# Two units of modulation columns later in attention, and one matmul for an input's hi and lo halves

## The chip, the cores and the metric

The kernel runs on one core of a Trainium2 chip, in one launch. The metric is device time in microseconds of that launch; the number for the kernel before is the median of three runs. One further execution was profiled, and all rows below come from it.

## What is computed

A sequence of 256 tokens of width 1024, in float32, goes through two blocks. The first has two layers; each is a mixer and an MLP with a squared ReLU, both modulated by a conditioning vector `c`. Layer 0 mixes by pooling, layer 1 by attention of 16 heads of 64 (with one key block of 256 it is causal attention with a relative-position bias):

```
mod = silu(c) @ w_mod[i] + b_mod[i];  sh1, sc1, g1, sh2, sc2, g2 = split(mod, 6)
h = rmsnorm(x) * (1 + sc1) + sh1
x = x + g1 * mixer(h)                       # layer 1: softmax(q k^T / 8 + bias) v, then @ w_o
h = rmsnorm(x) * (1 + sc2) + sh2
x = x + g2 * (relu(h @ w_up[i]) ** 2) @ w_down[i]          # d_ff = 4096
```

The second block has a gated delta rule and a forgetting attention side by side over 16 + 256 tokens, and then

```
h = h + (silu(f @ w_gate) * (f @ w_up)) @ w_down,   f = rmsnorm(h)      # d_ff = 2816
```

and a last norm.

## The kernel before

Every product is float32 made from two fp32r parts: an operand is split into hi (the rounded value) and lo (what is left). A product is then three matmuls into one PSUM tile, hi x hi, hi x lo, lo x hi; that is `mm3` (L261 to L264), and a triple below means these three. The weights are not split in memory: each megabyte comes as a raw DMA issued by SP (three raw buffers), ACT copies a piece of 128x1024 to hi (L245), DVE subtracts to lo (L251), five buffers each. The pieces are called wu (MLP up), wd (MLP down), wqk, wv, wo (attention), wgu and wfd (the last MLP's gate/up and down).

Where the weights are stationary (`weights_stationary`, `ws_steps`), the output is transposed: 128 output features by 256 tokens, built from eight 128-deep steps, so 24 matmuls of 256 columns. This is the form of MLP up, of gate/up and of q and k. In the second MLP up has seven such chunks of four feature tiles (an eighth is computed otherwise), gate/up ten. Two feature tiles lie in the two halves of one PSUM bank, `ps[:, q * S:(q + 1) * S]`; ACT's ReLU or SiLU and DVE's product read them there. The down products have 512 columns and follow one chunk behind.

The order of most instructions on each engine is set by a scheduler that plays the program against estimated times. In attention PE's order is written by hand: `InOrder` chains its matmuls, and a list of events with due times (`H_S`, `H_P`, `H_T`, ...) says beside which projection steps the scores of a pair of heads (`scores`), the transposes of the probabilities (`transposes`, PE tiles called pt, copied by ACT to pT) and the products with the values (`pv`) are issued. Softmax is on DVE (L1115 adds the bias and takes the maximum, L1117 negates it, L1119 and L1120 scale by the sum's reciprocal) and ACT (L1118, the exponential). At the end `until_head` flushes events between the steps of the output projection `wo(1, 0)`.

The modulation vectors are computed on DVE between other work. A unit of `pair_units` loads one megabyte wmc by SP and does two column reductions of 128x1024 (L444). In attention `riding()` is called after each projection and `ride(4)` issues one unit each time, as long as some are left.

The modulated input of an MLP is written by `boundary` into two tiles, one for hi and one for lo (`hl_tiles`).

Of the kernel before, what the change touches and what calls it, by code (L numbers as in the profile page):

```python
# [8 lines left out]
F32 = mybir.dt.float32  # L9
# [5 lines left out]
P = 128  # L15
# [18 lines left out]
B_FIRST = 4 * 128  # L34
B_PREV = 2 * B_FIRST
B_N = B_PREV + 4 * PADW
R_GATE = 2.0
H_S = 1.0
H_P = 2.8
H_L = 2.0  # L40
H_T = 6.5
H_V = 2.0
H_TL = 5.0
DELAY = 3
C_FEAT = 0.6
T2K = 8
R_LEFT = 10
# [60 lines left out]
V_BG, V_POOL = 15, 16  # L108


def interleave(main, filler, ratio=None):

    owed = 0.0
    for r in main:
        owed += r if ratio is None else ratio
# [42 lines left out]
def build(tc, a, out):  # L158
# [4 lines left out]
    with ctx:  # L163
# [13 lines left out]
        def mm_tile(name):  # L177
            return pmm.tile([P, 512], F32, tag="mm", name=name)
# [219 lines left out]
        def modulated_group(tp, scale, shift, hi, lo, c0, g, name, rows=P):  # L398

            for kt in (4 * g, 4 * g + 2):  # L400
                pair_split(pair_scaled(tp, scale, shift, kt, name, rows), hi, lo, c0, kt, rows)

        def hl_tiles(name, n):
            hi = big_tile(f"{name}_hi", F32R)[:, :KT * n].rearrange("p (k n) -> p k n", k=KT)
            lo = big_tile(f"{name}_lo", F32R)[:, :KT * n].rearrange("p (k n) -> p k n", k=KT)
            return hi, lo


        p1ctx = ExitStack()
# [3 lines left out]
        def t2k(name, bufs=T2K):  # L413
            return p1.tile([P, 512], F32, tag="t2k", name=name, bufs=bufs)
# [551 lines left out]
        def weights_stationary(w, h, ft, ps, c0=0, n=S):  # L966
            for _ in ws_steps(w, h, ft, ps, c0, n):
                pass

        def tm_steps(w, h, tok0, m, ps, grain=2):  # L970

            for kt in range(KT):
                mm3(ps, hl(h, kt, slice(tok0, tok0 + m)), w(kt * 512, 512), kt == 0, kt == KT - 1)
                if (kt + 1) % grain == 0:
                    yield
# [58 lines left out]
        def mlp(i, h, w0, wn, at, ahead=None):  # L1034


            def act2(src, name):
                n = src.shape[1]
                r = t2k(f"{name}r")[:, :n]
# [32 lines left out]
            def up(j):  # L1072
                w = ahead if i == 0 and j == NUP else split_chunk(a[f"w_up_{i}"][j - (1, NUP)[i == 0]], f"wu{i}{j}")
                ab = a_tile(j)
                for pr in range(2):
                    ps = mm_tile(f"up{i}{j}{pr}")
                    for q in range(2):
                        weights_stationary(w, h, 2 * pr + q, ps[:, q * S:(q + 1) * S])
# [4 lines left out]
                    split_act(ps, ab, slice(2 * pr, 2 * pr + 2), f"up{i}{j}{pr}")  # L1083
                return ab

            def split_act(ps, ab, ks, name):
                sq = act2(ps, name)
# [50 lines left out]
        def attention(i, h, w0, wn):  # L1138
# [5 lines left out]
            ohl = hl_tiles("att_o", S)  # L1144
            toep_ap = toep[:, :]
            st = {}

            def values(w, t):

# [30 lines left out]
                riding()  # L1180

            def riding():
                ride(4)
                if len(sums_due) > delay[0]:
                    sums_due.pop(0)()

# [67 lines left out]
            for pr in range(NH // 2):  # L1254
                hd = 2 * pr
                at = H_S + H_P * hd if hd < 12 else max(H_S + H_P * hd, 36.0 + H_S + H_L * (hd - 12))
                lag, by = (H_T, H_P) if hd < 12 else (H_TL, H_L)
                events += [(at, hd, scores, pr), (at + lag, hd, transposes, hd), (at + lag + by, hd + 1, transposes, hd + 1),
                           (at + lag + by + H_V, hd + 1, pv, pr)]
            events.sort(key=lambda e: e[0])  # L1260

            def beside(steps):
# [22 lines left out]
            for steps in todo[:2]:  # L1285
                for _ in steps:
                    pass
            for steps in todo[2:]:
                beside(steps)
            todo = all_projects(1)  # L1290
# [4 lines left out]
            wn.piece(0)  # L1295
            wn.piece(1)
            steps = wo(1, 0)
            for k in range(4):
                until_head(9 + 2 * k)
                next(steps)  # L1300
            next(steps, None)
            while sums_due:
                sums_due.pop(0)()
            pe = nc.tensor
# [18 lines left out]
        def mods(i, which):  # L1323
            return [modcol[i][:, c * KT:(c + 1) * KT] for c in (2 * which + 1, 2 * which)]
# [14 lines left out]
        ac, rest = attention(1, h, wv0, wu1)  # L1339
        while len(pending) > 4:  # L1340
            ride(4)
        h = boundary(ac, lambda: gates[1, 0], *mods(1, 1), hl_tiles("mlp1", S), 0, "mlp1", (rest, wu1))

        def wide_row(src, name):
            row = big_tile(name)[:, :D]
# [618 lines left out]

        ac, rest = drain(wo)

        fh = hl_tiles("f", S)
        boundary(ac, None, vcol(V_FFN), None, fh, 0, "f", (ahead(rest, wg0, fh, "gu00"), None))
        NJ = DFF2 // 256

# [3 lines left out]
        def swi(ps, name):  # L1974

            sg = t4("tmp", name, 6).rearrange("p h n -> p (h n)")
            act.activation(sg[:, :S], ps[:, :S], AF.Silu)
            vec.tensor_tensor(sg[:, S:], sg[:, :S], ps[:, S:], ALU.mult)
            return sg[:, S:]

        def gate_up_first():
            w = wg0
            ab = fa_tile(0)
            for t in range(2):
                if t == 0:
# [4 lines left out]
                sg = swi(ps, f"sg0{t}")  # L1990
                tp = tp_tile(f"gut{t}")
                for k in range(2):
                    pe.transpose(tp[:, k * P:(k + 1) * P], sg[:, k * P:(k + 1) * P], ident)
                ts = slice(t * P, (t + 1) * P)
                split_to(ab[:, 0, :, ts], ab[:, 1, :, ts], tp[:, :2 * P].rearrange("p (k n) -> p k n", k=2))
            return ab

        def gate_up(j):
            w = split_chunk(a["w_gu"][j - 1], f"wgu{j}")
            ab = fa_tile(j)  # L2000
            for ft in range(2):
                ps = mm_tile(f"gu{j}{ft}")
# [123 lines left out]
```

## Time and profile before

| | us |
|---|---|
| median of three runs | 940.36 (940.02 to 941.78) |
| the profiled execution | 940.04 |
| its span in the trace | 938.3 |
| attention | 256 to 358 |
| second MLP | 385 to 535 |
| second block's mixers | 535 to 750 |
| gate/up and down of the last MLP | 750 to 925 |

The span is the time from the first to the last recorded instruction; 1.7 us of the execution lie outside it. Stage limits are round numbers near where PE's work changes. PE is TensorE, PEld its weight loads, DVE VectorE, ACT ScalarE, SP SyncE. The start of a PE row is its issue; matmuls are pipelined, so the time that a matmul costs in a stream is the distance between starts, not the duration in its row. A row with x3 or x8 stands for several instructions; `[3.56 <-DVE ...]` is idle time of the engine just before the row and what ended it.

### The profile page before, as it was taken

The page shows a single profiled execution, that of the slowest core. Times are in us where ns is not written, and L with a number is a line of the kernel's source. Part 1 is how long each engine was busy: PE and PEld are TensorE (multiplying, and loading weights), DVE is VectorE, ACT ScalarE, POOL GpSimd, SP SyncE. Part 2 cuts the span into 40 slices and gives each one's busy share as a digit, 9 for nine tenths or more (in the row PEclk, how much of TensorE's full clock was granted, in tenths as well). Part 3 has the DMA queues.
Part 4 walks back from the last instruction along what each step waited for, and adds up shares of the span by engine and source line. Part 5 has one row for each costly group of instructions (what it writes and reads, how often), then busy time and mean ns, then how long its engine had stood idle before and what let it go on. Part 6 is the DMA issues. An engine that isn't in the chain of part 4 may idle for free.

```text
span 938.3 us, 15294 instructions
## 1 busy us (share of the span) xinstructions
PE 910.2 (97%) x6045; PEld 794.0 (85%) x6045; DVE 638.0 (68%) x1222; ACT 497.7 (53%) x881; POOL 12.5 (1%) x22
## 2 busy tenths in 40 slices
PE   6999999999998999999999999999999999999996
PEld 3668889988797977889999978899988799999995
DVE  1686898878797775875556667797558765555544
ACT  4476444445556663744455555766456554444442
POOL 0000000000000000000000001000000000000000
PEclk9999999999999999999999999999999999999999
DMA  9998899889285560875565545332112555555531
GB/s 364 420 420 316 317 358 353 340 320 342 93 331 197 169 225 0 299 274 180 197 221 180 198 152 169 121 120 92 46 46 91 201 195 198 187 184 180 180 136 45
DMA packets 34555, 198.31 MB, mean 211 GB/s; under 512 B 4186, under 2 KB 6818, under 8 KB 14002
## 3 DMA queue, kind: packets, MB, share of 16 engines
q1 hardware_dynamic: 34338, 197.27, 59.0%
q8 instruction: 47, 0.77, 0.3%
q14 instruction: 24, 0.20, 0.1%
q10 hardware_dynamic: 146, 0.08, 0.0%
HBM read 196.24 MB, written 1.09 MB: 210 GB/s over the span
## 4 chain that ended last, share of the span: by engine, by line
PE 87%; DVE 5%; DMA 3%; ACT 2%; issue 2%; POOL 0%; DVEq 0%; POOLq 0%; ACTq 0%
PE up L262 7%; PE up L264 6%; PE up L263 6%; PE dn L262 6%; PE dn L264 6%; PE dn L263 6%; PE gu L264 4%; PE gu L263 4%; PE gu L262 4%; PE qk L291 2%; PE fd L262 2%; PE fd L263 2%; PE fd L264 2%; PE cp L264 1%; PE cp L262 1%
## 5 line engine op out<-in xcount | busy, mean ns | idle before, releaser
L262 PE MATMUL up<-mlp_hi,wu_h 128*128 128x256 f32 x416 | 118.5, 285 | 0.0
L264 PE MATMUL up<-mlp_hi,wu_l 128*128 128x256 f32 x416 | 117.7, 283 | 0.6 <-DVE wu_l L251 0.6
L263 PE MATMUL up<-mlp_lo,wu_h 128*128 128x256 f32 x416 | 117.9, 284 | 0.0
L245 ACT ACTIVATE wd_h<-wd_r 128x1024 fp32r<-128x1024 f32 x58 | 61.3, 1060 | 66.2 <-PE up L263 42.1
L245 ACT ACTIVATE wu_h<-wu_r 128x1024 fp32r<-128x1024 f32 x58 | 60.8, 1063 | 65.9 <-PE dn L264 48.8
L251 DVE TENSOR_TENSOR wu_l<-wu_r,wu_h 128x1024 fp32r<-128x1024 f32 x58 | 70.3, 1221 | 36.9 <-ACT wu_h L245 36.6
L251 DVE TENSOR_TENSOR wd_l<-wd_r,wd_h 128x1024 fp32r<-128x1024 f32 x58 | 70.7, 1222 | 35.4 <-ACT wd_h L245 34.9
L262 PE MATMUL dn<-wd_h,a 128*128 128x512 f32 x232 | 91.1, 393 | 0.0
L263 PE MATMUL dn<-wd_l,a 128*128 128x512 f32 x232 | 90.9, 392 | 0.0
L262 PE MATMUL gu<-f_hi,wgu_h 128*128 128x256 f32 x320 | 90.7, 283 | 0.0
L264 PE MATMUL gu<-f_hi,wgu_l 128*128 128x256 f32 x320 | 90.6, 283 | 0.0
L263 PE MATMUL gu<-f_lo,wgu_h 128*128 128x256 f32 x320 | 90.6, 283 | 0.0
L264 PE MATMUL dn<-wd_h,a 128*128 128x512 f32 x232 | 90.4, 390 | 0.0
L251 DVE TENSOR_TENSOR wgu_l<-wgu_r,wgu_h 128x1024 fp32r<-128x1024 f32 x44 | 53.6, 1224 | 51.3 <-ACT wgu_h L245 51.3
L262 PEld LDWEIGHTS up<-mlp_hi,wu_h 128*128 128x128 f32 x416 | 79.7, 192 | 1.0 <-issue 0.5
L263 PEld LDWEIGHTS up<-mlp_lo,wu_h 128*128 128x128 f32 x416 | 79.7, 192 | 1.0 <-issue 0.5
L264 PEld LDWEIGHTS up<-mlp_hi,wu_l 128*128 128x128 f32 x416 | 79.7, 192 | 0.8 <-DVE wu_l L251 0.8
L245 ACT ACTIVATE wgu_h<-wgu_r 128x1024 fp32r<-128x1024 f32 x44 | 46.6, 1062 | 62.0 <-PE gu L263 29.4
L263 PEld LDWEIGHTS gu<-f_lo,wgu_h 128*128 128x128 f32 x320 | 61.4, 192 | 0.3
L262 PEld LDWEIGHTS gu<-f_hi,wgu_h 128*128 128x128 f32 x320 | 61.4, 192 | 0.4
L264 PEld LDWEIGHTS gu<-f_hi,wgu_l 128*128 128x128 f32 x320 | 61.4, 192 | 0.0
L264 PEld LDWEIGHTS dn<-wd_h,a 128*128 128x128 f32 x232 | 43.6, 188 | 10.0 <-issue 0.9
(792 smaller groups left out, 2269.7 us busy)
## 6 DMA issues: line engine op xcount, KB each, us to landing
wu_r<-in_w_up_dram SPq DMA_DIRECT2D x32, 1024.0 KB, 5.2
wd_r<-in_w_down_dram SPq DMA_DIRECT2D x32, 1024.0 KB, 6.4
wgu_r<-in_w_gu_dram SPq DMA_DIRECT2D x22, 1024.0 KB, 5.2
wmc<-in_w_modc_dram SPq DMA_DIRECT2D x16, 1024.0 KB, 6.9
wmg<-in_w_modg_dram SPq DMA_DIRECT2D x12, 1024.0 KB, 6.8
wfd_r<-in_w_fd_dram SPq DMA_DIRECT2D x11, 1024.0 KB, 4.8
wi_r<-in_w_in_dram SPq DMA_DIRECT2D x10, 1024.0 KB, 5.1
wms<-in_w_mods_dram SPq DMA_DIRECT2D x16, 512.0 KB, 9.9
```

Of the source, the lines that this page charges most:

```text
L245: act.activation(hi, r, AF.Copy)
L251: vec.tensor_tensor(lo, r, hi.bitcast(F32), ALU.subtract)
L262: pe.matmul(ps, l[0], r[0], start=first, stop=False)
L263: pe.matmul(ps, l[0], r[1], start=False, stop=False)
L264: pe.matmul(ps, l[1], r[0], start=False, stop=last)
L291: f(*a, **k)
```

## The change

The inputs of the second MLP and of the last MLP lie otherwise: `hl_beside` makes two tiles, one for the steps 0 to 3 and one for 4 to 7, in each of which a step's hi and lo stand beside each other, so that `both` is one operand of 512 columns. `ws_halves` then does per step one matmul of the weight's hi over both, and one of the weight's lo over hi. The sum of the two halves of the bank is made by `halves_sum` (ACT copies one half out, DVE adds the other). Each feature tile has a bank of its own, taken in turn from the pools mm and tp (`halves_tile`). The eighth chunk of MLP up, gate/up's first chunk and the first MLP stay as they were.

In attention `riding()` counts its calls and issues a unit only at those in `RIDES`; the transposes of the first pair get a later due time (`H_FIRST`), the pv of the sixth pair too (`H_VL`); at the end the order of `until_head` and of the steps of `wo(1, 0)` is another. An exponential of one column (`exp_table`) is added, and `R_GATE`, the ratio by which work is mixed into the second block's gating, becomes a list.

```diff
-R_GATE = 2.0
+R_GATE = (2.0, 2.0, 4.5, 1.5, 2.0, 3.0)
...
+H_VL = 3.5
+H_FIRST = 1.5
 H_TL = 5.0
 DELAY = 3
+RIDES = (1, 2, 3, 6, 8, 10)
...
+        def hl_beside(name, n):
+            tiles = [big_tile(f"{name}_{g}", F32R)[:, :KT * n].rearrange("p (k e n) -> p k e n", k=4, e=2) for g in range(2)]
+            return Part(tiles, 0), Part(tiles, 1)
+
+        def both(h, kt, cols):
+
+            return h[0].tiles[kt // 4][:, kt % 4, :, cols]
...
+        def ws_halves(w, h, ft, ps):
+
+
+            p2 = ps.rearrange("p (e n) -> p e n", e=2)
+            for kt in range(KT):
+                wl = w(ft * PIECE + kt * P, P)
+                pe.matmul(p2, wl[0], both(h, kt, slice(0, S)), start=kt == 0, stop=False)
+                pe.matmul(p2[:, 0], wl[1], h[0][:, kt], start=False, stop=kt == KT - 1)
+
+        def halves_tile(q, name):
+            return (mm_tile, tp_tile)[q](name)
+
+        def halves_sum(dst, ps):
+            act.activation(dst, ps[:, S:], AF.Copy)
+            vec.tensor_tensor(dst, ps[:, :S], dst, ALU.add)
...
+                        ps = halves_tile(q, f"up{i}{j}{pr}{q}")
+                        ws_halves(w, h, 2 * pr + q, ps)
+                        halves_sum(sums[:, q * S:(q + 1) * S], ps)
...
             def riding():
-                ride(4)
+                rode[0] += 1
+                if rode[0] in RIDES:
+                    ride(4)
                 if len(sums_due) > delay[0]:
                     sums_due.pop(0)()
...
+                lag += H_FIRST if pr == 0 else 0.0
                 events += [(at, hd, scores, pr), (at + lag, hd, transposes, hd), (at + lag + by, hd + 1, transposes, hd + 1),
-                           (at + lag + by + H_V, hd + 1, pv, pr)]
+                           (at + lag + by + (H_V, H_VL)[pr == 5], hd + 1, pv, pr)]
...
+            act.activation(work.tile([P, 1], F32, tag="psum", name="exp_table", bufs=4), ones[:, 0:1], AF.Exp)
...
-            for k in range(4):
-                until_head(9 + 2 * k)
-                next(steps)
-            next(steps, None)
+            for hd in (9, 11, 13):
+                until_head(hd)
+                if hd < 13:
+                    next(steps)
+
+            until_head(15)
+            for _ in range(3):
+                next(steps, None)
...
-        h = boundary(ac, lambda: gates[1, 0], *mods(1, 1), hl_tiles("mlp1", S), 0, "mlp1", (rest, wu1))
+        h = boundary(ac, lambda: gates[1, 0], *mods(1, 1), hl_beside("mlp1", S), 0, "mlp1", (rest, wu1))
...
-        fh = hl_tiles("f", S)
+        fh = hl_beside("f", S)
...
-            act.activation(sg[:, :S], ps[:, :S], AF.Silu)
-            vec.tensor_tensor(sg[:, S:], sg[:, :S], ps[:, S:], ALU.mult)
+            if len(ps) == 1:
+                act.activation(sg[:, :S], ps[0][:, :S], AF.Silu)
+                vec.tensor_tensor(sg[:, S:], sg[:, :S], ps[0][:, S:], ALU.mult)
+            else:
+                for q in range(2):
+                    halves_sum(sg[:, q * S:(q + 1) * S], ps[q])
+                act.activation(sg[:, :S], sg[:, :S], AF.Silu)
+                vec.tensor_tensor(sg[:, S:], sg[:, :S], sg[:, S:], ALU.mult)
...
-                ps = mm_tile(f"gu{j}{ft}")
+                ps = [halves_tile(q, f"gu{j}{ft}{q}") for q in range(2)]
                 for q in range(2):
-                    weights_stationary(w, fh, 2 * ft + q, ps[:, q * S:(q + 1) * S])
+                    ws_halves(w, fh, 2 * ft + q, ps[q])
```

How this moves instructions is shown at three places. The first is DVE at the first softmax of attention; wqk_l are weight pieces, wmc with modcol a unit of modulation columns, sm the scores of a head with its bias. Before the change:

```order
L251 TENSOR_TENSOR wqk_l_2804<-wqk_r_2801,wqk_h_2803 128x1024
L444 ISA wmc_2795,modcol_103<-wmc_2795,crow,vecs 128x1024
L444 ISA modcol_103 128x1
L444 ISA wmc_2795,modcol_103<-wmc_2795,crow,vecs 128x1024
L444 ISA modcol_103 128x1
L1115 ISA sm_2597,sm_m<-s_2589,toep_2587 128x128
L1115 ISA sm_m 128x1
L1115 ISA sm_2597,sm_m<-s_2589,toep_2587 128x256
L1115 ISA sm_m 128x1
L1115 ISA sm_2616,sm_m<-s_2592,toep_2590 128x128
```

The same place on DVE after the change:

```order
L254 TENSOR_TENSOR wqk_l_2801<-wqk_r_2798,wqk_h_2800 128x1024
L1168 ISA sm_2599,sm_m<-s_2591,toep_2589 128x128
L1168 ISA sm_m 128x1
L1168 ISA sm_2599,sm_m<-s_2591,toep_2589 128x256
L1168 ISA sm_m 128x1
L1168 ISA sm_2618,sm_m<-s_2594,toep_2592 128x128
L1168 ISA sm_m 128x1
L1168 ISA sm_2618,sm_m<-s_2594,toep_2592 128x256
L1168 ISA sm_m 128x1
L1170 TENSOR_SCALAR sm_nm<-sm_m 128x1 x3
L254 TENSOR_TENSOR wqk_l_2883<-wqk_r_2798,wqk_h_2882 128x1024
L1170 TENSOR_SCALAR sm_nm<-sm_m 128x1
```

The unit that stood ahead of the softmax's first four reductions is gone from there; the one that stood between the maxima and the scalings, a few rows further down, is gone too, and the next one comes behind the first scalings.

The second place is PE at the end of attention: wo is the output projection with its weight pieces wo_p, wo_h and wo_l, pt the last transposes, pv the last product with the values. Before the change:

```order
L291 MATMUL wo_3519<-wo_p_3656,att_o_hi 128x512 x2
L291 MATMUL wo_3519<-wo_p_3656,att_o_lo 128x512
L291 MATMUL wo_3518<-wo_p_3667,att_o_hi 128x512 x2
L291 MATMUL wo_3518<-wo_p_3667,att_o_lo 128x512
L291 MATMUL wo_3519<-wo_p_3667,att_o_hi 128x512 x2
L291 MATMUL wo_3519<-wo_p_3667,att_o_lo 128x512
L291 MATMUL pt_3676<-ident,sm_3565 128x128 x3
L291 MATMUL pv_3682<-pT_3635,att_v 64x256
L291 MATMUL pv_3682<-pT_3680,att_v 64x256
L291 MATMUL pv_3682<-pT_3635,att_v 64x128
L291 MATMUL pv_3682<-pT_3680,att_v 64x128
L291 MATMUL wo_3518<-wo_h_3689,att_o_hi 128x512
```

The same place on PE after the change:

```order
L294 MATMUL wo_3514<-wo_p_3658,att_o_hi 128x512 x2
L294 MATMUL wo_3514<-wo_p_3658,att_o_lo 128x512
L294 MATMUL pt_3667<-ident,sm_3560 128x128 x3
L294 MATMUL pv_3673<-pT_3637,att_v 64x256
L294 MATMUL pv_3673<-pT_3671,att_v 64x256
L294 MATMUL pv_3673<-pT_3637,att_v 64x128
L294 MATMUL pv_3673<-pT_3671,att_v 64x128
L294 MATMUL wo_3513<-wo_p_3682,att_o_hi 128x512 x2
L294 MATMUL wo_3513<-wo_p_3682,att_o_lo 128x512
L294 MATMUL wo_3514<-wo_p_3682,att_o_hi 128x512 x2
L294 MATMUL wo_3514<-wo_p_3682,att_o_lo 128x512
L294 MATMUL wo_3513<-wo_h_3691,att_o_hi 128x512
```

Before, the step with wo_p_3667 stands ahead of the last transposes and the last step right behind pv; after, one step (wo_p_3658) stands ahead of them, and the steps with wo_p_3682 and wo_h_3691 behind.

The third is PE at the seam of gate/up (gu) and the down product (fd); f is the input, fa the activations. Before the change:

```order
L262 MATMUL gu_8343<-f_hi,wgu_h_8374 128x256
L263 MATMUL gu_8343<-f_lo,wgu_h_8374 128x256
L264 MATMUL gu_8343<-f_hi,wgu_l_8375 128x256
L262 MATMUL fd_7948<-wfd_h_8409,fa_8115 128x512
L263 MATMUL fd_7948<-wfd_l_8410,fa_8115 128x512
L264 MATMUL fd_7948<-wfd_h_8409,fa_8115 128x512
L262 MATMUL fd_7949<-wfd_h_8409,fa_8115 128x512
```

The same seam after the change:

```order
L1003 MATMUL gu_8278<-f_7601,wgu_h_8301 128x512
L1004 MATMUL gu_8278<-f_7601,wgu_l_8302 128x256
L265 MATMUL fd_7796<-wfd_h_8332,fa_8082 128x512
L266 MATMUL fd_7796<-wfd_l_8333,fa_8082 128x512
L267 MATMUL fd_7796<-wfd_h_8332,fa_8082 128x512
L265 MATMUL fd_7797<-wfd_h_8332,fa_8082 128x512
```

A triple of 256 columns has become a pair of 512 and 256; the down product's triples are as they were.

## Rows read from the trace of the kernel before

**Rows 1.** The profile page, section 4: the chain that ended last, by engine.

```profile
PE 87%; DVE 5%; DMA 3%; ACT 2%; issue 2%; POOL 0%; DVEq 0%; POOLq 0%; ACTq 0%
```

**Rows 2.** By stage: length, busy PE PEld DVE ACT POOL (count), granted clock, DMA share, GB/s.

```profile
256.00:358.00 102.00, 96.54 (x721) 84.81 (x720) 77.36 (x231) 61.81 (x132) 0.00 (x0) 0.98 0.61 212
...
385.00:535.00 150.00, 150.00 (x982) 137.21 (x981) 95.52 (x116) 76.57 (x97) 0.53 (x1) 1.00 0.65 218
...
750.00:925.00 175.00, 175.00 (x1226) 164.55 (x1225) 91.07 (x108) 77.88 (x106) 0.00 (x0) 1.00 0.51 169
```

**Rows 3.** What PE waited for, 255 to 372 us: total, times, longest.

```profile
PE pt L291 <- DVE sm_nm L1117: 3.6, 1, 3.6
PE pv L291 <- ACT pT L1218: 1.2, 1, 1.2
...
PE wo L291 <- ACT att_o_hi L982: 0.5, 1, 0.5
```

**Rows 4.** Finer windows of attention, same columns.

```profile
256.00:282.00 26.00, 25.92 (x199) 24.18 (x198) 25.57 (x47) 15.33 (x20) 0.00 (x0) 1.00 0.81 306
...
287.00:290.00 3.00, 3.00 (x16) 3.00 (x15) 3.00 (x13) 1.62 (x6) 0.00 (x0) 0.50 1.02 371
290.00:330.00 40.00, 40.00 (x338) 36.75 (x338) 27.52 (x100) 26.73 (x64) 0.00 (x0) 1.00 0.45 141
```

**Rows 5.** PE in attention: start us, duration, engine, line, operation [idle before].

```profile
273.40 0.93 PE L291 MATMUL s<-att_k,att_q 64*128 64x128 f32 x8
...
280.92 0.93 PE L291 MATMUL s<-att_k,att_q 64*128 64x128 f32 x8
...
282.48 0.28 PE L291 MATMUL qk<-att_hi,wqk_l 128*128 128x256 f32 x1
286.32 1.08 PE L291 MATMUL pt<-ident,sm 128*128 128x128 f32 x3 [3.56 <-DVE sm_nm L1117]
...
297.43 0.37 PE L291 MATMUL qk<-att_hi,wqk_h 128*128 128x256 f32 x1
```

**Rows 6.** DVE in attention, same columns.

```profile
274.98 1.27 DVE L444 CUSTOM_DVE_ANT_0 wmc<-wmc,crow,vecs 128x1024 f32<-128x1024 f32 x1
...
277.39 0.28 DVE L1115 CUSTOM_DVE_ANT_0 sm<-s,toep 128x128 f32<-128x128 f32 x1
...
285.99 0.27 DVE L1120 TENSOR_SCALAR sm<-sm,sm_rs 128x128 f32<-128x128 f32 x1
```

**Rows 7.** PE in gate/up and its down product.

```profile
839.68 0.28 PE L262 MATMUL gu<-f_hi,wgu_h 128*128 128x256 f32 x1
839.79 0.28 PE L263 MATMUL gu<-f_lo,wgu_h 128*128 128x256 f32 x1
...
849.75 0.28 PE L262 MATMUL gu<-f_hi,wgu_h 128*128 128x256 f32 x1
...
851.07 0.28 PE L264 MATMUL gu<-f_hi,wgu_l 128*128 128x256 f32 x1
851.19 0.40 PE L262 MATMUL fd<-wfd_h,fa 128*128 128x512 f32 x1
851.43 0.40 PE L263 MATMUL fd<-wfd_l,fa 128*128 128x512 f32 x1
```

**Rows 8.** PE in the down product of the second MLP.

```profile
513.78 0.39 PE L262 MATMUL dn<-wd_h,a 128*128 128x512 f32 x1
...
517.86 0.39 PE L262 MATMUL dn<-wd_h,a 128*128 128x512 f32 x1
```

**Rows 9.** Groups by shape, 750 to 925 us: count, busy, mean ns, idle before.

```profile
L251 DVE TENSOR_TENSOR wgu_l<-wgu_r,wgu_h 128x1024 fp32r<-128x1024 f32 x40 | 48.8, 1224 | 50.4 <-ACT wgu_h L245 50.4
...
L1978 DVE TENSOR_TENSOR sg<-sg,gu 128x256 f32<-128x256 f32 x22 | 9.1, 414 | 0.7 <-ACT sg L1977 0.7
...
L1977 ACT ACTIVATE sg<-gu 128x256 f32<-128x256 f32 x22 | 8.1, 370 | 1.9 <-PE gu L264 1.9
```

**Rows 10.** ACT near the end of attention.

```profile
336.48 2.01 ACT L245 ACTIVATE wo_p<-wo_r 128x1024 fp32r<-128x1024 f32 x2 [2.38 <-DMA wo_r<-in_w_o_dram]
```

More of the change, by code (lines that the diff above doesn't have):

```diff
@@ L108, with interleave @@
 V_BG, V_POOL = 15, 16
-def interleave(main, filler, ratio=None):
+def interleave(main, filler, ratios):
     owed = 0.0
-    for r in main:
-        owed += r if ratio is None else ratio
+    for n, _ in enumerate(main):
+        owed += ratios[n]
         while owed >= 1.0:
@@ L401, in modulated_group, with __init__, __getitem__ @@
                 pair_split(pair_scaled(tp, scale, shift, kt, name, rows), hi, lo, c0, kt, rows)
+        class Part:
+            def __init__(self, tiles, e):
+                self.tiles, self.e = tiles, e
+            def __getitem__(self, at):
+                p, k, *c = at
+                c = c[0] if c else slice(None)
+                if isinstance(k, slice):
+                    g = k.start // 4
+                    k = slice(k.start - 4 * g, k.stop - 4 * g)
+                else:
+                    g, k = k // 4, k % 4
+                return self.tiles[g][p, k, self.e, c]
         def hl_tiles(name, n):
@@ L1034, in mlp, with act2 @@
         def mlp(i, h, w0, wn, at, ahead=None):
-            def act2(src, name):
+            def act2(src, name, r=None):
                 n = src.shape[1]
-                r = t2k(f"{name}r")[:, :n]
+                if r is None:
+                    r = t2k(f"{name}r")[:, :n]
                 act.activation(r, src, AF.Relu)
@@ L1075, in up @@
                 for pr in range(2):
-                    ps = mm_tile(f"up{i}{j}{pr}")
+                    sums = t2k(f"up{i}{j}{pr}s") if i else mm_tile(f"up{i}{j}{pr}")
                     for q in range(2):
-                        weights_stationary(w, h, 2 * pr + q, ps[:, q * S:(q + 1) * S])
+                        if not i:
+                            weights_stationary(w, h, 2 * pr + q, sums[:, q * S:(q + 1) * S])
+                            if q:
+                                ride(R_LEFT)
+                                if j >= R_FROM:
+                                    ride(R_LEFT)
+                            continue
+                        ps = halves_tile(q, f"up{i}{j}{pr}{q}")
+                        ws_halves(w, h, 2 * pr + q, ps)
+                        halves_sum(sums[:, q * S:(q + 1) * S], ps)
                         if q:
@@ L1082, in up @@
                                 ride((R_LEFT, 0)[i])
-                    split_act(ps, ab, slice(2 * pr, 2 * pr + 2), f"up{i}{j}{pr}")
+                    split_act(sums, ab, slice(2 * pr, 2 * pr + 2), f"up{i}{j}{pr}")
                 return ab
             def split_act(ps, ab, ks, name):
-                sq = act2(ps, name)
+                sq = act2(ps, name, ps if i else None)
                 h_ap = ab[:, 0, ks].rearrange("p k n -> p (k n)")
@@ L1146, in attention @@
             st = {}
+            rode = [0]
             def values(w, t):
@@ L1976, in swi @@
             sg = t4("tmp", name, 6).rearrange("p h n -> p (h n)")
-            act.activation(sg[:, :S], ps[:, :S], AF.Silu)
-            vec.tensor_tensor(sg[:, S:], sg[:, :S], ps[:, S:], ALU.mult)
+            if len(ps) == 1:
+                act.activation(sg[:, :S], ps[0][:, :S], AF.Silu)
+                vec.tensor_tensor(sg[:, S:], sg[:, :S], ps[0][:, S:], ALU.mult)
+            else:
+                for q in range(2):
+                    halves_sum(sg[:, q * S:(q + 1) * S], ps[q])
+                act.activation(sg[:, :S], sg[:, :S], AF.Silu)
+                vec.tensor_tensor(sg[:, S:], sg[:, :S], sg[:, S:], ALU.mult)
             return sg[:, S:]
@@ L1989, in gate_up_first @@
                     token_major(w, fh, t * P, P, ps)
-                sg = swi(ps, f"sg0{t}")
+                sg = swi([ps], f"sg0{t}")
                 tp = tp_tile(f"gut{t}")
```

## The prediction

> **What bounds the kernel now.** I read the chain of work that ended last first [rows 1]: 87% of it is TensorE (PE), so what counts is how many columns PE streams and where it stands still; VectorE (DVE), the DMAs and ScalarE (ACT) own the chain only in pieces. The table by stages [rows 2] then says where: in the second MLP (385 to 535 us) and in gate/up (750 to 925 us) PE has no idle microsecond, while DVE is busy 95.52 of 150 and 91.07 of 175, ACT 76.57 and 77.88, and the DMA share is 0.65 and 0.51. There only less PE work helps, and there is room on the other engines. In attention (256 to 358 us) PE is busy 96.54 of 102: what is lost there is waiting. The table of waits [rows 3] puts a name to it: one stop of 3.6 us before a transpose of probabilities (pt), 1.2 us before a product with the values (pv), 0.5 us before the output projection (wo). Last, the finer windows [rows 4]: after the 3.6 us stop the granted clock is 0.50 for 3 us, that is the lower of the two levels (1.2 against 2.4 GHz), in which 16 matmuls took 3.00 us.
>
> **Merged matmuls, MLP1 up and gate/up.** Three matmuls of 256 columns per weight tile become one of 512 and one of 256. The columns are the same, 768; what goes is one matmul and its weight load. 7 chunks x 4 x 8 triples in MLP1 and 10 x 4 x 8 in gate/up make 224 + 320 = 544 fewer. What one matmul costs beyond its columns stands in starts: in gate/up eleven pitches from 849.75 to 851.07 us give 0.1200 us for 256 columns [rows 7], in MLP1's down product eighteen pitches from 513.78 to 517.86 give 0.2267 for 512 [rows 8]. A triple is 0.3600, the pair would be 0.3467: 13 ns less, x 544 = 7.2 us. No row of before alternates the two shapes with two weights, so it is bounded by the changes of shape [rows 7]: the first 512 behind a 256 took 0.24 (851.19 to 851.43), the first 256 behind a 512 took 0.11 (839.68 to 839.79). If each 512 costs 0.24 and the 256 keeps 0.12, the pair is 0.36 and nothing is gained; if the 512 keeps 0.2267 and the 256 costs 0.11, it is 0.337, and 12.7 us are gained; both edges together give 0.35, 5.4 us. I take 7.0, next to the two long runs.
>
> The Trainium skill, "TensorE: Matmul & The Clock Gate", section "Back-to-back issue gap", gives the gap of warm matmuls as columns over 2.4 GHz and 2.5 ns more. By that a matmul taken out brings 2.5 ns, an estimate of 1.4 us in all. The rows disagree: they show 13 ns over the columns at both sizes, and the measured rows decide.
>
> The price of the merge is that the hi and lo halves are now apart in a whole PSUM bank and must be added: one ACT copy of 128x256 and one DVE addition for each of (7 + 10) x 4 = 68 output tiles. The nearest rows are 370 ns (ACT from PSUM, 128x256) and 414 ns (DVE, same size) [rows 9]: 68 x 0.37 = 25 us on ACT and 68 x 0.41 = 28 us on DVE, spread over 325 us in which ACT has 170 and DVE 138 us idle [rows 2]. They also stand behind each other with the weight pieces (DVE 1.22 us each [rows 9]). Each of the four tiles of a chunk has a bank of its own, and a bank is written again only a chunk later: three other tiles of 16 matmuls (2.8 us each) and the 24 matmuls of the down product (5.4 us) lie between, some 13 us for a copy and an addition. Cost on the path: nothing; if the cover goes, up to 2 us for a chunk (a copy, an addition, a piece). At the start of MLP1 the first down matmuls now stand nearer to the first sums: 0 to 1 us, taken as 0.3.
>
> **Modulation columns later.** A unit is two column reductions on DVE, about 2.4 us (274.98 to 277.39) [rows 6]. Before, the first softmax stood behind such a unit: its scores left PE at 274.3 (273.40 and 0.93) [rows 5], the DVE reached them at 277.39, a second unit lay in the middle of the softmax, and the first scaled probabilities came at 285.99, while PE had run dry: last qk at 282.48, transpose at 286.32. After, no unit lies there, so the softmax starts at about 275.0. Even at its old length of 8.6 us (277.39 to 285.99) it would end at 283.6; without the unit inside it is nearer 6.2 us, 281.2.
>
> **First transposes later.** With H_FIRST the transpose stands behind 24 qk matmuls after the second scores instead of 6. Those scores end at 281.85 (280.92 and 0.93); 24 x 0.12 later is 284.7. The probabilities are there 1.1 us before even on the long reckoning, so the stop of 3.56 us goes. With it goes the slow clock: 16 matmuls in 3.00 us instead of 16 x 0.12 = 1.92 is 1.1, and half of the 1.08 us of the transpose beside it, 0.5. Sum 5.2. From PE's side: the same 60 qk matmuls, three transposes, the next scores and pv are done at 297.43 before [rows 5], and would stand at about 292.2. Lower end 2 (a weight piece late instead: PE asks for the pieces sooner), upper end 5.6.
>
> The moved units come back at calls 6, 8 and 10: two land on DVE between 290 and 335 us. There DVE is busy 27.52 of 40 us [rows 4], so 2 x 2.4 = 4.9 us go into 12.5 idle ones, ahead of scalings whose transposes stand some 4 us later. Cost 0; if they come too late, up to 2.4 each.
>
> **End of attention.** The 1.2 us wait of pv is for ACT's copy pT, which stood behind two weight splits (those waited 2.38 us for their DMA) and four exponentials [rows 3, 10]; now the copy stands ahead of the exponentials: -1.1. The last wo step no longer comes right behind the last pv: the six matmuls of the step before it (6 x 0.23 = 1.4 us) cover ACT's copy of the head's output, so the 0.5 us wait of wo goes. Against it, the softmax of the last pair now stands on DVE ahead of the scalings of the pair before, and its ACT copies behind two more weight splits: 0.4, between 0 and 1.5. Net -1.2.
>
> **Without effect.** The activation named exp_table is put by the scheduler at the kernel's start, not before attention; a table load still stands before the first exponential. The list R_GATE leaves the instructions of its section in the same order. Both 0.
>
> Sum against the profiled execution: 940.04 - 7.0 + 0.3 - 5.2 - 1.2 = 926.9 us. That execution lies 0.3 under the median of 940.36, so no correction is made.
>
> **Rivals.** A, the pair costs as much as the triple (0.24 + 0.12): 926.9 + 7.0 = 933.9. For it speaks the row of 0.24, against it that long runs settle at 0.2267.
>
> D, the pair keeps most of the fixed cost, since every 512 now follows a 256 and every 256 a 512: 0.24 for the one and 0.115, between 0.11 and 0.12, for the other make 0.355, 5 ns less than the triple, 2.7 us in all: 926.9 + 4.3 = 931.2. For it speak the edges, against it that the second edge showed 0.11. The rule of the Trainium skill named above would come near this, by its estimate of 1.4 us.
>
> B, attention gives its gain back: the later units or the weight splits at the end hold up transposes that PE now reaches 5 us sooner, two stops of some 2.4 us: 931.7. For it: DVE is busy 25.57 of 26 us up to 282 and all of 287 to 290 [rows 4], so only the units that left make room. Against it: the idle time on DVE after 290 [rows 4].
>
> C, slower: every chunk waits for its sums. Place: a weight piece on ACT and DVE queued behind a copy that waits for PE, in each of 17 chunks. Price: 0.37 + 0.41 + 1.22 = 2.0 us a chunk, 34 us, so 961. It decides from 13.1 / 17 = 0.8 us a chunk, where it eats the other gains. Against it: ACT and DVE are half idle there and PE waits for neither today.
>
> E, nothing happens: A together with a first softmax that stays late; 940.
>
> **How the numbers follow.** Mine 66% (its own range 923.5 to 930), A 8, D 7, B 9, C 5, E 5. The time is that of the likeliest, 926.9. The range of 8 in 10 goes from 922.5 (a merge worth 11 us) to 933.0, which takes in B and D. A measurement of this kernel tells 0.2%, 1.9 us: faster by more than that holds for mine, A, D and B, 0.90; E is the same, 0.05; C slower, 0.05.
>
> **What would show it.** In the later profile: starts of a 512 and a 256 in gate/up 0.347 us apart as a pair (A: 0.36, D: 0.355); no stop before the first transpose, and no window of clock 0.50 behind it; MLP1 and gate/up without waits of PE, some 3 and 4 us shorter; pv and wo of the last heads without their 1.2 and 0.5. I am wrong if PE waits for an addition on DVE or for a weight piece in those two stages, or if a new stop of over 2 us stands in attention.

## The result and the profile after

The changed kernel takes 928.37 us (median of 4 runs, 927.33 to 931.61), the kernel before in the same session 940.98: a ratio of 0.9872, interval 0.9845 to 0.9899. The forecast was 926.9, for the execution that was profiled; that of the changed kernel took 928.71, its span is 926.9. The sum came out within 2 us, its terms did not: the merge brought half of what was forecast for it, attention somewhat more, and the two errors cancel in part. That the sum came so near is luck to that extent.

The view for this is the distance between starts of PE's rows at the same places of both programs. The first 247 us, in which the DMA share is 0.91 in both, end at times that differ by up to 2.7 us among the profiled runs of this study, so that stages are compared by their own lengths: attention from the first matmul of v to the last of wo, MLP1 from there to the last of its down product, gate/up from its first matmul to the last of the final down product.

| us, from starts of PE rows | attention: to scores of the 3rd pair | from there to the end | MLP1 | mixers | gate/up, down |
|---|---|---|---|---|---|
| before | 47.9 | 76.7 | 184.3 | 186.1 | 188.0 |
| after | 42.5 | 74.1 | 182.8 | 186.6 | 186.1 |
| difference | -5.4 | -2.6 | -1.5 | +0.5 | -1.9 |

With -0.3 of the start this is -11.3, the difference of the spans (938.3 and 926.9) within a tenth.

In attention, the finer windows of after (columns as in [rows 4]) show no stretch of low clock:

```profile
256.00:282.00 26.00, 25.70 (x198) 24.02 (x197) 23.50 (x48) 16.37 (x25) 0.00 (x0) 1.00 0.81 298
282.00:287.00 5.00, 5.00 (x44) 5.00 (x43) 4.54 (x19) 4.12 (x12) 0.00 (x0) 1.00 0.82 268
287.00:290.00 3.00, 3.00 (x27) 2.54 (x26) 3.00 (x10) 2.02 (x4) 0.00 (x0) 1.00 0.88 325
290.00:330.00 40.00, 40.00 (x338) 36.30 (x339) 32.22 (x110) 26.32 (x63) 0.00 (x0) 1.00 0.56 184
```

The second of them was, before the change:

```profile
282.00:287.00 5.00, 1.32 (x9) 0.92 (x9) 5.00 (x23) 3.00 (x12) 0.00 (x0) 0.99 0.98 328
```

There PE was busy 1.32 us of 5 and is now busy throughout; DVE was full and has 0.46 us free. From 287 to 290 PE has 27 matmuls where it had 16 [rows 4], and DVE is full as before. What PE waited for from 255 to 372 us, against [rows 3]:

```profile
PE up L265 <- DVE mlp L398: 0.8, 1, 0.8
PE mlp_tp L593 <- DVE mlp_xn L589: 0.7, 1, 0.7
PE s L294 <- ACT att_k L1233: 0.3, 1, 0.3
```

The waits of pt (3.6), pv (1.2) and wo (0.5) are gone; the 0.8 is the start of MLP1, which now lies within the window (before, the same wait of 0.8 stood behind 372). PE's rows at the first softmax (start, duration), against [rows 5]:

```profile
280.81 0.93 PE L294 MATMUL s<-att_k,att_q 64*128 64x128 f32 x8
284.64 0.49 PE L294 MATMUL pt<-ident,sm 128*128 128x128 f32 x3
287.85 0.49 PE L294 MATMUL pt<-ident,sm 128*128 128x128 f32 x3
```

and DVE's, against [rows 6]:

```profile
273.52 1.22 DVE L254 TENSOR_TENSOR wqk_l<-wqk_r,wqk_h 128x1024 fp32r<-128x1024 f32 x1
274.65 0.28 DVE L1168 CUSTOM_DVE_ANT_0 sm<-s,toep 128x128 f32<-128x128 f32 x1
...
279.62 0.73 DVE L1173 TENSOR_SCALAR sm<-sm,sm_rs 128x128 f32<-128x128 f32 x3
...
285.50 1.28 DVE L471 CUSTOM_DVE_ANT_0 wmc<-wmc,crow,vecs 128x1024 f32<-128x1024 f32 x1
```

The softmax begins right behind a weight piece at 274.65 (forecast 275.0), the first head is scaled by 280.35 (279.62 and 0.73; forecast 281.2, at the latest 283.6), and the transposes come at 284.64 (forecast 284.7) without a wait: four microseconds to spare.

In gate/up, PE's rows, against [rows 7]:

```profile
847.12 0.40 PE L1003 MATMUL gu<-f,wgu_h 128*128 128x512 f32 x1
847.36 0.28 PE L1004 MATMUL gu<-f,wgu_l 128*128 128x256 f32 x1
847.47 0.40 PE L1003 MATMUL gu<-f,wgu_h 128*128 128x512 f32 x1
847.70 0.28 PE L1004 MATMUL gu<-f,wgu_l 128*128 128x256 f32 x1
847.82 0.40 PE L1003 MATMUL gu<-f,wgu_h 128*128 128x512 f32 x1
848.06 0.28 PE L1004 MATMUL gu<-f,wgu_l 128*128 128x256 f32 x1
848.18 0.40 PE L1003 MATMUL gu<-f,wgu_h 128*128 128x512 f32 x1
```

Three pairs take 1.06 us, 0.3533 each: the 512s cost 0.23 to 0.24, above the 0.2267 of a long run [rows 8], the 256s 0.11 to 0.12. Over all pairs of gate/up the means are 0.2356 and 0.1169. Against a triple's 0.360 a pair of 0.3533 saves 6.7 ns, x 544 = 3.6 us; the stages show 1.5 + 1.9 = 3.4.

The added sums, grouped by shape in gate/up (count, busy us, mean ns, idle before), cost what [rows 9] gave, and none of PE's waits from 385 to 925 us is for one of them:

```profile
L1011 DVE TENSOR_TENSOR sg<-gu,sg 128x256 f32<-128x256 f32 x40 | 16.7, 418 | 0.0
...
L1010 ACT ACTIVATE sg<-gu 128x256 f32<-128x256 f32 x40 | 14.6, 366 | 1.0 <-PE gu L1004 1.0
```

### The profile page after: what moved, and what is told of

It is laid out like the page before. It is cut to its first block, busy times and chain, and to the rows that moved or that the text cites. A ratio compares the mean times of both kernels' runs of the same rounds, so it can differ in the third digit from the quotient of the medians.

```text
span 926.9 us, 14379 instructions
## 1 busy us (share of the span) xinstructions
PE 903.4 (97%) x5501; PEld 762.5 (82%) x5501; DVE 661.1 (71%) x1290; ACT 518.0 (56%) x950; POOL 12.7 (1%) x22
## 4 chain that ended last, share of the span: by engine, by line
PE 85%; DMA 5%; DVE 5%; ACT 2%; issue 2%; SPq 0%; POOL 0%; DVEq 0%; POOLq 0%; ACTq 0%
PE gu L1003 8%; PE dn L267 6%; PE dn L265 6%; PE dn L266 6%; PE up L1003 6%; PE gu L1004 4%; PE qk L294 4%; PE up L265 4%; PE up L267 4%; PE up L266 4%; PE up L1004 3%; DMA wms<-in_w_mods_dram 2%; PE fd L265 2%; PE fd L267 2%; PE fd L266 2%
## 5 line engine op out<-in xcount | busy, mean ns | idle before, releaser
L1003 PE MATMUL gu<-f,wgu_h 128*128 128x512 f32 x320 | 113.5, 398 | 0.0
L1004 PE MATMUL gu<-f,wgu_l 128*128 128x256 f32 x320 | 89.8, 281 | 0.0
L1003 PE MATMUL up<-mlp,wu_h 128*128 128x512 f32 x224 | 79.3, 397 | 0.0
L1003 PEld LDWEIGHTS gu<-f,wgu_h 128*128 128x128 f32 x320 | 60.1, 188 | 14.7
L1004 PE MATMUL up<-mlp,wu_l 128*128 128x256 f32 x224 | 62.9, 281 | 0.0
L1004 PEld LDWEIGHTS gu<-f,wgu_l 128*128 128x128 f32 x320 | 60.4, 189 | 0.4
L265 PE MATMUL up<-mlp_hi,wu_h 128*128 128x256 f32 x192 | 55.2, 288 | 0.0
L267 PE MATMUL up<-mlp_hi,wu_l 128*128 128x256 f32 x192 | 54.3, 284 | 0.6 <-DVE wu_l L254 0.6
L266 PE MATMUL up<-mlp_lo,wu_h 128*128 128x256 f32 x192 | 54.3, 283 | 0.0
L266 PEld LDWEIGHTS dn<-wd_l,a 128*128 128x128 f32 x232 | 43.6, 188 | 9.2 <-issue 0.5
```

The source lines that it names most:

```text
L265: pe.matmul(ps, l[0], r[0], start=first, stop=False)
L266: pe.matmul(ps, l[0], r[1], start=False, stop=False)
L267: pe.matmul(ps, l[1], r[0], start=False, stop=last)
L1003: pe.matmul(p2, wl[0], both(h, kt, slice(0, S)), start=kt == 0, stop=False)
L1004: pe.matmul(p2[:, 0], wl[1], h[0][:, kt], start=False, stop=kt == KT - 1)
```

## The experiments

The diffs of this section are shortened to the lines that matter. Theory: the merge saves 6.7 ns a pair and not 13, because every 512 stands behind a 256; the stop at the first softmax has gone with the late units and the late transposes; the end of attention brought more than its 1.2 us. Rivals are the forecast's own sizes, and for the merge that the sums or the two-part operand cost the missing half. "Changed" below means the changed kernel. Stage lengths are worked out as in the table above.

**The two halves of the change apart.**

```diff
# attn_only: the changed kernel with
-        h = boundary(..., hl_beside("mlp1", S), ...)       fh = hl_beside("f", S)
+        h = boundary(..., hl_tiles("mlp1", S), ...)        fh = hl_tiles("f", S)
-    ws_halves(...); halves_sum(...)
+    weights_stationary(w, h, 2 * pr + q, sums[:, q * S:(q + 1) * S])      # gate/up likewise
# merge_only: the changed kernel with
-RIDES = (1, 2, 3, 6, 8, 10)      H_FIRST = 1.5      H_VL = 3.5
+RIDES = (1, 2, 3, 4, 5, 6)       H_FIRST = 0.0      H_VL = 2.0
# and the loop over until_head(9 + 2 * k) as before
```

> The new attention without the merge: MLP up and gate/up are triples of 256 columns again, everything else as in the changed kernel. By the starts in the trace of after a pair costs 0.3535 us and a triple 0.3600, 6.5 ns each, 544 of them: 3.5 us, so about 932 where the changed kernel has 928.4 (theory: the merge was worth half of the forecast, attention more). Rival, the forecast's 7 us from the merge: 935.4. In the trace attention should end 8 us earlier than before, and MLP1 and gate/up should take what they took before.

> The merge with the attention of before (units ride with every call, first transposes and the end of attention as before). Theory: 3.5 us under the kernel before, about 937; rival (forecast): 7 us under it, about 933.5. If the two parts are independent, the gains of this run and of the new attention alone add up to that of the whole change, 12.

Measured: attention alone 932.96 us, ratio 0.9921 (0.9909 to 0.9933), 7.4 us under the kernel before; the merge alone 937.78, 0.9972 (0.9960 to 0.9984), 2.6 us under. Together 10 of the 12; the rest is within the intervals. By stages the merge alone shortens MLP1 to 182.7 and gate/up to 186.1, as the changed kernel does (182.8, 186.1), and attention alone leaves them at 184.3 and 188.0. In the merge's own run a part of this is hidden: its attention is as before, but the stop at the first softmax was longer in that execution, and attention took 125.7 us where the kernel before took 124.6:

```profile
287.09 1.14 PE L294 MATMUL pt<-ident,sm 128*128 128x128 f32 x3 [4.28 <-DVE sm_nm L1170]
```

So the merge is worth 3.5 us, not 7. Attention is worth 7.4 by the medians (interval 6.3 to 8.6) and 7.5 by its stage (117.05 after 124.57); the forecast's 6.4 lies at the lower end of that.

**Shapes in runs.** Eight 512s, then eight 256s, in each feature tile:

```diff
+            wl = [w(ft * PIECE + kt * P, P) for kt in range(KT)]
             for kt in range(KT):
-                wl = w(ft * PIECE + kt * P, P)
-                pe.matmul(p2, wl[0], both(h, kt, slice(0, S)), start=kt == 0, stop=False)
-                pe.matmul(p2[:, 0], wl[1], h[0][:, kt], start=False, stop=kt == KT - 1)
+                pe.matmul(p2, wl[kt][0], both(h, kt, slice(0, S)), start=kt == 0, stop=False)
+            for kt in range(KT):
+                pe.matmul(p2[:, 0], wl[kt][1], h[0][:, kt], start=False, stop=kt == KT - 1)
# grouped2: the same over two feature tiles, sixteen and sixteen
```

> The changed kernel, but in each feature tile the eight matmuls of 512 columns come first and then the eight of 256, so shapes change twice instead of sixteen times; same columns, same number of matmuls. Theory (the missing gain is paid at each change of shape): pitches of 0.227 and 0.120 inside the runs, 14 of 16 edges gone, 68 x 0.05 = 3.2 us less, about 925.2. Rival 1 (the 512-column matmul over the two halves is dear by itself, by its operand): starts stay at 0.236, the time at 928.4. Rival 2 (a weight's lo piece is late): slower, with waits of PE for DVE.

> As the kernel with eight 512s and then eight 256s, but over two feature tiles: sixteen 512s, then sixteen 256s. In the trace of that kernel a tile of eight pairs took 2.793 us where eight plain pairs are 2.773, the excess lying in the first six 512s behind a 256. Theory (the excess is paid once per change of shape and dies out): 68 x 0.010 = 0.7 us less than with eight, about 926.3, and the later 512s of each run at 0.227. Rival 1 (the excess goes with each 512 in some other pattern): no gain, 927. Rival 2 (the sums of two tiles now come together and hold up a bank or the down product): slower, with waits of PE.

Measured: 927.04 us, 0.9866 (0.9847 to 0.9886), and for sixteen 926.92, 0.9850 (0.9830 to 0.9871). The intervals overlap with the changed kernel's; the traces do not leave it open. PE's rows with eight (a row holds the eight of a run; the first run stands behind 512s of the down product, the others behind 256s):

```profile
844.06 1.98 PE L1003 MATMUL gu<-f,wgu_h 128*128 128x512 f32 x8
845.88 1.11 PE L1005 MATMUL gu<-f,wgu_l 128*128 128x256 f32 x8
846.83 2.00 PE L1003 MATMUL gu<-f,wgu_h 128*128 128x512 f32 x8
848.67 1.12 PE L1005 MATMUL gu<-f,wgu_l 128*128 128x256 f32 x8
849.62 2.00 PE L1003 MATMUL gu<-f,wgu_h 128*128 128x512 f32 x8
```

and with sixteen:

```profile
850.00 3.82 PE L1011 MATMUL gu<-f,wgu_h 128*128 128x512 f32 x16
853.66 2.08 PE L1016 MATMUL gu<-f,wgu_l 128*128 128x256 f32 x16
```

Behind 256s, eight 512s take 1.84 us (848.67 - 846.83) where eight at 0.2267 are 1.81; sixteen take 3.66 (853.66 - 850.00) where sixteen are 3.63. The excess, 0.03, is the same for both: it is paid once behind a change from 256 to 512, over the first five matmuls, and not with each one. The run behind the down product's 512s pays nothing: 1.82 (845.88 - 844.06), on the average of the ten such runs 1.815, where the 28 runs of gate/up behind 256s all take 1.84. A pair costs 0.349 in runs of eight (2.79 us for eight) against 0.3533 alternating. MLP1 comes to 181.9 and gate/up to 184.4 with eight, 181.6 and 184.0 with sixteen: the merge is then worth 6.0 and 6.6 us, the latter near the 7.0 of the forecast. The two-part operand is not dear by itself. The saving forecast for eight and eight, 3.2 us, came to 2.6 by the stages.

**The first softmax.**

```diff
# rides_early         -RIDES = (1, 2, 3, 6, 8, 10)     +RIDES = (1, 2, 3, 4, 5, 6)
# first_early         -H_FIRST = 1.5                   +H_FIRST = 0.0
# both_early          both lines
```

> The changed kernel with the units of modulation columns at the first six calls again (RIDES 1 to 6), the later first transposes kept. Theory A (each of the two measures alone is enough, since the forecast's long reckoning put the probabilities at 283.6 and the transposes at 284.7): 0 to 1 us slower, 928.4 to 929.4, no stop before the first transposes. Theory B (the units are what made the stop): a stop of some 1 to 3 us and the slow clock behind it are back, 930.5 to 933.

> The changed kernel with the first transposes at their old place, six qk matmuls behind the second scores, the units late. Theory A (the probabilities are scaled at 280.35 in the trace of after, before the old place at about 282.4): no stop, 928.4 plus or minus 1. Theory B (the later place is what took the stop away): a stop of 1 us or more at the first transposes, and the slow clock, 930 to 932.

> Both undone: units at the first six calls and first transposes at their old place; merge and end of attention as changed. Both theories: the stop of 3.6 us before the first transposes and the stretch of clock 0.50 are back, 5.2 to 5.5 us slower than the changed kernel, about 933.7. If it stays at 928.4, neither made the stop.

Measured: 930.08 us, 0.9886 (0.9871 to 0.9900), with the units early; 928.64, 0.9869 (0.9855 to 0.9884), with the transposes early; 935.56, 0.9945 (0.9930 to 0.9959), with both. Only the last has the stop. Its first transposes and the window behind them:

```profile
285.80 1.13 PE L294 MATMUL pt<-ident,sm 128*128 128x128 f32 x3 [4.12 <-DVE sm_nm L1170]
```

```profile
286.00:290.00 4.00, 4.00 (x19) 3.76 (x19) 4.00 (x16) 2.37 (x9) 0.00 (x0) 0.50 0.95 341
```

From the start of v to the scores of the third pair the two single ones take 42.3 us, both together 49.0, after 42.5. So theory A holds for the time: each measure alone takes the whole stop, and having both adds nothing there.

For the later transposes alone it holds with little to spare, and not by the reckoning that was given: that one started the softmax at 275.0, which needs the late units. With the units early it starts at 278.31, its first head is scaled by 285.21 (284.86 and 0.35), and the transposes come at 285.73:

```profile
278.31 0.29 DVE L1168 CUSTOM_DVE_ANT_0 sm<-s,toep 128x128 f32<-128x128 f32 x1
...
284.86 0.35 DVE L1173 TENSOR_SCALAR sm<-sm,sm_rs 128x256 f32<-128x256 f32 x1
...
287.04 1.26 DVE L471 CUSTOM_DVE_ANT_0 wmc<-wmc,crow,vecs 128x1024 f32<-128x1024 f32 x1
```

The second unit, which stood between the maxima and the scalings before and does so in both_early (279.35), stands behind the scalings here, at 287.04: with the transposes due later, the scheduler moved it. Without that move, and with the old 8.6 us from the first maximum to the first scaling, the scaling would start at 286.9, an estimate, behind the place of the transposes.

What the early units cost (1.7 us by the medians, 1.3 in the end of attention by the trace) lies elsewhere: pv of the fifth pair takes 1.35 to 1.84 us from its start to the next matmul in the four kernels with early units and 0.80 to 0.93 in all with late ones. Before the change its row was

```profile
329.88 1.42 PE L291 MATMUL pv<-pT,att_v 128*64 128x256 f32 x8
```

where 0.87 is the plain length. Another 0.9 is at the pv of the seventh pair; whether the units' order or a late transfer made that is not separated (see the next group). both_early lost 7.2 us against the changed kernel, more than forecast: the stop is 0.6 longer than before (a DMA of a unit came 0.45 us late for DVE there), the slow stretch lasts longer as well (the clock granted from 290 to 294 is 0.89, before it was 1.00 from 290 on [rows 4]), and the cost of the early units comes on top. The three profiled kernels with the stop took 47.9, 49.0 and 49.4 us to the third scores, so the stop and what follows it cost 5.4 to 6.9 us, not one fixed amount.

**The end of attention, and the small edits.**

```diff
# tail_old
-            for hd in (9, 11, 13): ...      until_head(15); three steps       H_VL = 3.5
+            for k in range(4): until_head(9 + 2 * k); next(steps)             H_VL = 2.0
# small_off
-R_GATE = (2.0, 2.0, 4.5, 1.5, 2.0, 3.0)
+R_GATE = (2.0,) * 6
-            act.activation(..., name="exp_table", ...)
```

> The changed kernel with the end of attention as before: the flushes and the steps of the output projection in the old order, and pv of the sixth pair at its old due time. Theory (from PE's starts: the products with the values cost 10.0 us before and 7.25 after): 2.6 us slower than the changed kernel, 931, with the waits of 1.2 us before pv and 0.5 before wo back. Rival (forecast, -1.2 net): 929.6.

> The changed kernel without the exponential named exp_table and with the one ratio 2.0 in place of the list R_GATE. Theory: neither does anything, 928.4 within a microsecond. Rival: the list moves matmuls in the second block and is worth 1 us or more there, or the table load is the reason why the first exponentials come in time.

tail_old: 930.17 us, 0.9897 (0.9881 to 0.9912). The median lies where the two expectations meet, but its profiled run began 1.6 us late, and the stretch from the third scores to the end is 74.4 us against 74.1: with the old order only the 0.5 us wait of wo is back, not that of pv. So the new order of flushes is worth some 0.4 (the kernel called minimal below, which has the old order too, has the same wait of 0.5), the expected 2.6 is not borne out by the trace, and since the four times of tail_old (929.76 to 931.42) lie among those of the changed kernel (927.33 to 931.61), the medians do not settle it. The wait of pv went with something else, and ACT's rows say with what. In the changed kernel, against [rows 10]:

```profile
330.37 2.01 ACT L248 ACTIVATE wo_p<-wo_r 128x1024 fp32r<-128x1024 f32 x2 [0.78 <-DMA wo_r<-in_w_o_dram]
332.29 0.47 ACT L1274 ACTIVATE pT<-pt 128x384 f32<-128x384 f32 x1
```

in tail_old:

```profile
331.68 2.01 ACT L248 ACTIVATE wo_p<-wo_r 128x1024 fp32r<-128x1024 f32 x2 [0.68 <-DMA wo_r<-in_w_o_dram]
333.60 0.47 ACT L1274 ACTIVATE pT<-pt 128x384 f32<-128x384 f32 x1
```

and with the units early:

```profile
332.04 2.01 ACT L248 ACTIVATE wo_p<-wo_r 128x1024 fp32r<-128x1024 f32 x2 [2.23 <-DMA wo_r<-in_w_o_dram]
...
335.71 0.46 ACT L1274 ACTIVATE pT<-pt 128x384 f32<-128x384 f32 x1
```

Where the units are late, the scheduler has put one of two pieces of the next weights (wu_m) further back on ACT and the copy pT right behind wo_p; where they are early, four exponentials stand between. It is the late units that move the copy, by the scheduler's order, and not the flushes. The later due time of that pv (`H_VL`) would do too: with the units early the copy ends at 336.17 (335.71 and 0.46), and pv, which now starts at 337.53, does not wait for it.

small_off: 930.59 us, 0.9898 (0.9873 to 0.9923), but its profiled execution took 928.68, with the stages MLP1 and gate/up equal to a tenth and the mixers 0.5 shorter (186.1, where the profiled runs with the list have 185.9 to 186.6). In attention the same instructions stand in the same order, and the trace has one new wait, that of PE for the scaling of a later pair:

```profile
337.19 0.70 PE L294 MATMUL pt<-ident,sm 128*128 128x128 f32 x3 [1.65 <-DVE sm L1173]
```

It comes from a DMA: ACT's wo_p waited 2.49 us for the weights:

```profile
331.03 2.01 ACT L248 ACTIVATE wo_p<-wo_r 128x1024 fp32r<-128x1024 f32 x2 [2.49 <-DMA wo_r<-in_w_o_dram]
```

That DMA was issued at 324.22 and let ACT go on 6.8 us later; in the changed kernel 325.27 and 5.1. With equal instructions the end of attention thus varies by 1.5 us with one transfer. Six of the profiled kernels have the same order of instructions in attention (the changed one, attn_only, grouped, grouped2, small_off, sums_twice): the transfer takes 5.0 to 6.8 us in them, and the stretch from the third scores to the end 74.1 to 75.6. I read the two edits as worth nothing; the timed runs alone would not exclude 2 us.

**The price of the sums.**

```diff
         def halves_sum(dst, ps):
             act.activation(dst, ps[:, S:], AF.Copy)
+            act.activation(dst, ps[:, S:], AF.Copy)
             vec.tensor_tensor(dst, ps[:, :S], dst, ALU.add)
+            vec.tensor_copy(dst, dst)
```

> The changed kernel with the price of the sums doubled: ACT's copy of each half bank is done twice and DVE copies each sum once more onto itself, 68 more operations on each engine. Theory (the sums lie beside PE's work and cost nothing on the path): 928.4 within a microsecond, no wait of PE for ACT or DVE in MLP1 or gate/up. Rival (a part of the merge's missing 3.5 us is the sums' chain): slower by what the sums cost now, some 3 us, 931 to 932.

Measured: 933.65 us, 0.9930 (0.9908 to 0.9951). The number is the rival's, the place is not: MLP1 takes 183.0 (after 182.8), gate/up 186.0 (186.1), the mixers between them 190.4 (186.6). What PE waited for from 385 to 925 us:

```profile
PE u_tp L593 <- DVE u_xn L589: 2.6, 1, 2.6
PE f_tp L593 <- DVE f_xn L589: 0.4, 1, 0.4
PE fc L1536 <- DVE logf L1529: 0.3, 1, 0.3
```

The stop lies at the seam behind MLP1. With other work on ACT and DVE the scheduler put the end of the down product in another order. The down product itself ends 1.2 us later than in the changed kernel (547.0 and 545.8), but DVE gets its first tile 3.9 us later. The changed kernel:

```profile
538.98 0.69 DVE L541 TENSOR_TENSOR u_t<-dn,gate 128x512 f32<-128x512 f32 x1 [1.31 <-PE dn L267]
```

and this one:

```profile
542.91 0.69 DVE L541 TENSOR_TENSOR u_t<-dn,gate 128x512 f32<-128x512 f32 x1 [4.03 <-PE dn L267]
```

and the norm, whose result PE needs, comes late by as much. So the doubled sums add 0.2 us in MLP1 and nothing in gate/up, but the added work changed an order elsewhere. The expectation was wrong on the time and right on the stages.

**Only what is needed.**

```diff
# minimal: the grouped kernel (eight and eight) with
-H_FIRST = 1.5      H_VL = 3.5      exp_table      R_GATE list      new end of attention
+H_FIRST = 0.0      H_VL = 2.0      no exp_table   R_GATE 2.0       end of attention as before
```

> The kernel before with only two things: the units of modulation columns late, and the merged matmuls in groups of eight. First transposes, pv of the sixth pair and the end of attention at their old places, no exp_table, one R_GATE ratio. Theory (the late units alone remove the stop at the first softmax, and by the order of ACT's weight pieces also the waits before pv): within a microsecond of the grouped kernel's 927.0. Rival (the later transposes and the new end of attention carry 2 us or more of the gain): 929 or more.

Measured: 926.69 us, 0.9845 (0.9825 to 0.9864); the theory, as to the time. Of the waits, that of pv is 0.2 here and that of wo 0.5 as before, so the late units do not take them all. Attention takes 117.4 from v to wo (after 116.6, grouped 117.1), MLP1 181.9, gate/up 184.4. Late units and a merge in runs carry the whole gain; this kernel, the grouped ones and the changed one cannot be told apart by their times alone.

## Why the prediction was right, and where it was not

The time and the range held: 928.4 in 922.5 to 933.0. The places of the gain were right; that the sum came within 2 us is in part luck, since the merge's shortfall of 3.5 us met a larger gain in attention. By its steps:

- **Merged matmuls, -7.0: measured -3.5.** This is the term that was mis-sized. The working set the pair at 0.3467 from two long runs and put the edge of 0.24 aside, "next to the two long runs". In the changed kernel there are no long runs: each 512 stands behind a 256, and the edge is the rule. Rival D, which priced exactly that at 0.355 and gave it 7%, was 2 ns off. The runs of eight and sixteen show that the excess belongs to the change of shape, and those behind the down product, which are without it, show it too.
- **The rule of the Trainium skill** ("TensorE: Matmul & The Clock Gate", "Back-to-back issue gap"), 2.5 ns for each matmul taken out, 1.4 us: measured are 6.7 ns alternating and 12 ns in runs of sixteen (6.6 us for 544). The Trainium skill gives this formula, in the same section, for a single matmul by itself, which the forecast did not say, and for a stream with weight loads some 131 ns a matmul at 512 columns. The rows show 226.7 ns there and 120.0 at 256 [rows 7, 8], so the trace agrees with neither figure.
- **Sums hidden, 0:** right. Start of MLP1, +0.3: not seen; MLP1 is shorter by 1.5, which is 224 x 6.7 ns.
- **First softmax, -5.2: measured -5.4** against this execution of the kernel before, up to -6.9 against the others with the stop. Place and times as forecast. But the forecast priced two measures as one chain; each would have done alone. Its own numbers said so for the late units: probabilities at 281.2, ahead even of the old place of the transposes behind the qk of 282.48. For the later transposes they did not: what makes them enough is the unit that the scheduler moved.
- **End of attention, -1.2: measured -2.6 in that run,** and -1.1 to -2.6 over the six kernels with the same order there. The waits named did go. The reason given for pv, the copy ahead of the exponentials, holds in the rows, but the late units put it there and not the new order of the end, which is worth some 0.4. The counter-term of +0.4 is not seen in that run, but PE waits 0.7 us in grouped, 0.8 in attn_only and 1.6 in small_off for scalings that DVE does behind the first reductions of the last pair, which is the wait that the forecast named. A term was left out: the hidden wait in pv of the fifth pair (row of 1.42 us where 0.87 is the plain length), which went with the early units. Together the products with the values took 10.0 us before and 7.25 after, each from its start to the next matmul; the last one keeps its long row (1.51). How much of the 2.6 is a transfer's luck stays open, since equal orders gave 74.1 to 75.6 us.
- **exp_table and R_GATE, 0:** not contradicted, and not shown to better than 2 us by the timed runs.
- **The later units on DVE, 0:** right; DVE is busy 32.2 of 40 us from 290 on (27.5 before), and PE waits for none of them.

## What to carry to other kernels

When matmuls of two lengths replace three of one, price them in the order in which they will stand: a first row behind a change of shape is not an edge to be put aside if every row is one. Put equal shapes in runs. Before two measures against one stop are added up, ask whether each alone removes it, and by which order of instructions; and where a scheduler sets the order, compare stage by stage, since an edit can cost time in a place that it does not touch.

## What was not expected of the hardware

Where 512 and 256 columns alternate, a 512 costs 0.236 us to the next start and not 0.227, and the 256 behind it 0.117 and not 0.120. In a run of 512s behind 256s the excess is 0.03 us in all, over the first five, whether eight or sixteen follow; behind other 512s there is none. Which part of the engine it is, no run here tells. And one transfer of a megabyte took 5.0 to 6.8 us from its issue until its reader started, in the same place of the same program order.
